# Spacing the side work of a hybrid decoder's first projection, and starting one output norm a product later

## The chip, the cores and the metric

The kernel runs on one core of a Trainium2 chip. The metric is the device time of one execution in microseconds. Three runs of the kernel before gave 2690.6 us as the median (2689.2 to 2692.82).

## What is computed

One inference step of a decoder layer, in fp32, for a prompt of 2048 tokens and 8 samples of 8 tokens each (64 more columns), with model width 1024. Cut to what matters here:

```python
mod = silu(c) @ w_ada + b_ada                      # 6 vectors of shifts, scales, gates
h = rmsnorm(x, norm_mix_w) * (1 + sc1) + sh1
qkv, z, b, a, sq, sk, sv = split(h @ w_in)
qkv = silu(causal_dwconv(qkv, width 4))            # q, k, v of the gated DeltaNet
q, k = l2norm(q) * 128 ** -0.5, l2norm(k)
mix = concat(gated_delta(q, k, v, z, b, a), window_attention(sq, sk, sv))
x = x + g1 * (mix @ w_out)
h = rmsnorm(x, norm_ffn_w) * (1 + sc2) + sh2
gate, up = split(causal_dwconv(h @ w_up, width 3) + conv_b)
x = x + g2 * ((silu(gate) * up) @ w_down)
y = rmsnorm(x, final_norm_w)
```

`l2norm(t)` is `t * rsqrt(sum(t * t) + EPS)`. The outputs are y for both groups, and the new states and caches.

## The kernel before

Channels lie on the 128 partitions and tokens along the free dimension. Every large product is done with each operand split into a high half `hi` (rounded to a shorter fp32 form) and a low half `lo` (the remainder): three matmuls, hi x hi, hi x lo and lo x hi, make one step (`gemm_steps`, L319; the matmul is L324). For a weight tile, ScalarE casts the high half (L315) and another engine subtracts to get the low one (L316). The tokens are treated in two halves, `hf` = 0 and 1, each in three blocks `bi` of up to 384 columns.

**Order of the work.** The program writes generators. `beside(steps, filler, share)` (L334) runs one step of side work, then `share` steps of a filler, which is a projection; `lockstep` (L343) takes one step of each of its chains in a pass. The Tile framework then schedules the instructions by this priority and by its own simulated times, so that an engine's final order can differ from the program's. Each engine runs its queue in order. All loads and stores are issued on SP's queue. `tc.issue_after(loads[-1])` keeps a load behind the last weight load.

**The first input projection** (the end of the main part, up to `first.close()`). Two of its 22 row tiles, m = 0 and 1, are made during the start. Then `inproj(0, h, ic, range(2, 12))` is the filler: 10 tiles x 3 blocks x 8 steps = 240 steps, over five PSUM banks in turn. The first 28 steps run alone; then `beside(tasks, filler, SHARE[3])` with `SHARE[3]` = 8.0 adds two chains in lockstep:

- `ada_cols` (L171), eight groups of four loads `wada` of 512 KB, each with 64 small matmuls (L181), a copy by ScalarE (L184) and transposes (L188), two steps a group; then `weight_sums` of six units (L1577), three steps each: loads of `suv`, four VectorE sums, stores to `ws_d` that the down projection reads much later.
- `bias_tables` (eight steps), `gates` (eleven steps), and three times `x_rstd` (L269): the squares of the second token half are summed in `xacc` (four steps), then `token_rstd` (L205) adds over the partitions with a matmul into `ss_ps` (L214), VectorE and GpSimd make 1/rms (`rsq` L142, `rtok` L143), VectorE makes one diagonal matrix `dg` for each 128 tokens (L218), and after a `yield` a matmul with ones spreads them over the partitions (`rb_ps`, L222), which ScalarE copies (L224).

The evacuation `in_evac` (L571) of a tile m < 12 runs the convolution (`conv_block`, L515; the taps are L531 on VectorE) and `silu2` (L542):

```python
nc.scalar.activation(t, x, AF.Tanh, scale=0.5)                          # L545
nc.vector.scalar_tensor_tensor(x, t, 1.0, x, ALU.add, ALU.mult)         # L546
```

It gives twice the silu. `front` (L622), which normalises q and k for each chunk of 128 tokens, undoes the factor 2: it adds 4 EPS to the sums of squares and halves one of its norms. Tiles 12 to 21 of the first half (z, and the attention's q, k, v) are a later filler, beside the first chunks. For odd m, GpSimd makes the low half of an input weight, for even m VectorE.

**Down** (`down_phase`, L1604). A Strassen-like scheme of seven products (`DOWN`: A11 B11, S2 T2, S3 T3, S1 T1, S4 B22, A22 T4, A12 B21), done for the first and the second part (`ip` = 0 and 1) of both token halves, which are the groups 2 and 1. A product takes eleven steps i of four accumulators; four or eight of the eight PSUM banks, in the rotating list `free`, hold them. T2 and T4 are made on the fly from two loads each (`tr`, `tx`, L1668); the others are loaded as they are. `norm` (L1693) is the final RMSNorm of one group of columns: `token_rstd`, then the products with 1/rms by VectorE (L1717) and GpSimd (L1714), and the stores of y. One step of it is taken after each step i from 1 to 7 of the product that it lies beside. For `ip` = 0, group 2's norm is made after product j = 4 and runs beside j = 5 (A22 T4), in the banks `free[4:6]`; for `ip` = 1 its arguments are kept in `late` and it runs one product later, in `free[-2:]`. Group 1's norms are late already.

Of the kernel before, what the change touches and what calls it, by code (L numbers as in the profile page):

```python
# [17 lines left out]
AF = mybir.ActivationFunctionType  # L18
# [11 lines left out]
NCH = L // P  # L30
# [4 lines left out]
EPS = 1e-6  # L35
# [6 lines left out]
PW, SW = L // 4, L // 8  # L42
# [52 lines left out]
def kernel(  # L95
# [5 lines left out]
    nc = tc.nc  # L101
# [103 lines left out]
    def token_rstd(accs, n, dst, pool, bank):  # L205


        ps = bank("ss_ps")
        r = pool.tile([P, 4], F32, tag="rtok", name="rtok")

        cuts = [min(t, n - P) for t in range(0, n, P)]
        for j, t in enumerate(cuts):
            for i, a in enumerate(accs):
                nc.tensor.matmul(ps[:, j:j + 1], a[:, t:t + P], ones[:, 0:1], start=i == 0, stop=i == len(accs) - 1)  # L214
        rsqrt(pool, r[:, :len(cuts)], ps[:, :len(cuts)], 1.0 / D, len(cuts))
        dg = pool.tile([P, len(cuts), P], F32, tag="sq", name="dg", bufs=2)
        for j, t in enumerate(cuts):
            nc.vector.tensor_scalar_mul(dg[:, j], ident, r[:, j:j + 1])  # L218
        yield True
        bp = bank("rb_ps")  # L220
        for j, t in enumerate(cuts):
            nc.tensor.matmul(bp[:, t:t + P], ones, dg[:, j], start=True, stop=True)  # L222
        if dst is not None:
            nc.scalar.copy(dst[:, :n], bp[:, :n])  # L224
        yield True
# [43 lines left out]
    def x_rstd(hf, bi, rB, pool, bank):  # L269

        c0, n = HALVES[hf][bi]
        acc = pool.tile([P, HB[0]], F32, tag="xacc", name="xacc", bufs=2)[:, :n]
        for k in range(KT):
            x = pool.tile([P, HB[0]], F32, tag="xst", name="xst", bufs=5)[:, :n]
            with tc.issue_after(loads[-1]):
                nc.sync.dma_start(x, I["xT"][k, :, c0:c0 + n])
            nc.scalar.activation(x if k else acc, x, AF.Square)
            if k:
                nc.gpsimd.tensor_tensor(acc, acc, x, ALU.add)
            if k % 2:  # L280
                yield True
        yield from token_rstd([acc], n, rB, pool, bank)

    def first_rstd(bi, xs, rB, pool, bank, eng):

# [24 lines left out]
    def load_split(src, eng=None, out=None):  # L310
        return split(load_raw(src), eng, out)
# [37 lines left out]
    def chain(*gens):  # L349
        for g in gens:  # L350
            yield from g
# [5 lines left out]
    def project(ms, src, load, hb, hf, evac, after=None, freed=None, tags=("acc",), turn=(2, 2), third=None, w0=None):  # L357


        order = list(pairs(ms, turn))  # L360
        new = [m for i, (m, _) in enumerate(order) if m not in [x for x, _ in order[:i]]]
        first = max(2, turn[0])
        w = {m: w0 if w0 and not i else (load, third)[i == 2](m) for i, m in enumerate(new[:first])}
        new = new[first:]
        last = {bi: i for i, (_, bi) in enumerate(order)}
        for i, (m, bi) in enumerate(order):
            ps = bank(src, tags[i % len(tags)])
            yield from gemm_steps(ps, w[m], hb[bi], HALVES[hf][bi][1])
            if bi == 2 and new:
                w[new[0]] = load(new[0])  # L370
                new.pop(0)
            evac(m, bi, ps)
            if bi == 2 and after:
                after(m)
            if freed and last[bi] == i:
                freed(bi)
# [138 lines left out]
    def conv_block(ps, n, np_, hist, state, w, bias, dst):  # L515
# [23 lines left out]
            nc.gpsimd.tensor_copy(state, sb[:, :, NT_S:])  # L539
        return rb  # L540

    def silu2(x, rb):  # L542

        t = rb[:, :x.shape[1]]
        nc.scalar.activation(t, x, AF.Tanh, scale=0.5)  # L545
        nc.vector.scalar_tensor_tensor(x, t, 1.0, x, ALU.add, ALU.mult)  # L546
# [24 lines left out]
    def in_evac(hf, bi, m, ps, ic):  # L571
        c0, n = HALVES[hf][bi]
        np_ = n - LS if c0 + n == LT else n
        ev = evp[0].tile([P, 512], F32, tag="cv", name="ev", bufs=evp[2])[:, :n]
        if m < 12:
            o = ic["out"]
            rb = conv_block(ps, n, np_, o[:, m, 0:3], b8(o[:, m, 3:27]), ic["cw"][:, m], None, ev)
            silu2(ev, rb)
        elif m < 16:
            nc.scalar.activation(ev, ps[:, :n], AF.Tanh, scale=0.5)  # L580
            nc.vector.scalar_tensor_tensor(ev, ev, 1.0, ps[:, :n], ALU.add, ALU.mult)
            nc.gpsimd.tensor_scalar(ev, ev, ic["dnw"], 1.0, ALU.mult, ALU.mult)
        elif m < 20:
            nc.scalar.mul(ev, ps[:, :n], -0.125)
        else:
            nc.scalar.copy(ev, ps[:, :n])
        nc.sync.dma_start(proj[m, :, c0:c0 + n], ev)
        if m == 20 and c0 + n == LT:
            nc.sync.dma_start(O["p_swa_k"], ev[:, np_ - P:np_])
            nc.sync.dma_start(O["s_swa_k_new"], ev[:, np_:])  # L590

    def inproj(hf, h, ic, ms, **kw):
        return project(ms, "in_ps", lambda m: load_split(I["w_inT"][m], nc.gpsimd if m % 2 else nc.vector), h, hf,
                       lambda m, bi, ps: in_evac(hf, bi, m, ps, ic), **kw)


# [25 lines left out]
    def front(c, d, pool, rows=P):  # L622
# [15 lines left out]
        ss = pool.tile([P, H, 2], F32, tag="ss", name="ss")  # L638
        kq_ps = []
        for i in range(2):  # L640
            ps = heads(bank(f"kq_ps{i}", "fr"))
            kq_ps.append(ps)
            for h in range(H):
                nc.tensor.transpose(ps[:rows, h, :], kq[:, h, i, :], ident)
            for h in range(H):
                jk = pool.tile([P, P], BF16, tag="junk", name="junk", bufs=1)
                nc.scalar.activation(jk[:rows], ps[:rows, h, :], AF.Square, accum_out=ss[:rows, h, i:i + 1])
            yield True

        nc.vector.tensor_scalar_add(ss[:rows], ss[:rows], 4 * EPS)  # L650
        nr = pool.tile([P, H, 2], F32, tag="nr", name="nr", bufs=1 if smp else 3)
        nc.gpsimd.tensor_tensor(nr[:rows], ss[:rows], halves[:rows], ALU.pow)
        bn = pool.tile([P, 2, H], F32, tag="bn", name="bn")
# [10 lines left out]
        Dc = pool.tile([P, H, rows], F32, tag="gm", name="Dc", bufs=2)  # L664
        nc.scalar.activation(Dc[:rows], d_ps[:rows, :H * rows].rearrange("p (h i) -> p h i", h=H), AF.Exp)
        nc.gpsimd.tensor_tensor(Dc[:rows], Dc[:rows], over_h(tle, rows), ALU.mult)
        nc.vector.tensor_scalar_mul(nr[:rows, :, 0], nr[:rows, :, 0], 0.5)
        nc.vector.tensor_scalar_mul(nr[:rows, :, 1], nr[:rows, :, 1], float(128.0 ** -0.5))
        yield True
        v_ps = bank("v_ps", "fr")  # L670
# [906 lines left out]
    def weight_sums(units, pool):  # L1577

        tt = nc.vector.tensor_tensor
        cut = lambda t: (t[:, :D // 2], t[:, D // 2:])  # L1580
        for i in units:
            uv = pool.tile([P, 2, D], F32, tag="suv", name="suv", bufs=1)
            for x, k in enumerate((K1[i], K2[i])):
                with tc.issue_after(loads[-1]):
                    nc.sync.dma_start(uv[:, x], I["w_downT"][k])
            (a11, a21), (a12, a22) = cut(uv[:, 0]), cut(uv[:, 1])
            yield True
            tt(a22, a21, a22, ALU.add)
            tt(a21, a11, a21, ALU.subtract)
            tt(a11, a22, a11, ALU.subtract)  # L1590
            tt(a12, a12, a11, ALU.subtract)
            yield True
            for x in range(2):
                nc.sync.dma_start(ws_d[KH * x + i], uv[:, x])
            yield True
# [8 lines left out]
    def down_phase(ds, dr, pd):  # L1604
# [4 lines left out]
        free = [pd.tile([P, 512], F32, tag=f"d{i}", name="dn_ps", bufs=1) for i in range(8)]  # L1609
        free = [free[i] for i in (3, 4, 2, 1, 0, 5, 6, 7)]  # L1610
# [116 lines left out]
        finish = None  # L1727
        for q in range(Q):
            ip, j = divmod(q, ND)
            wn, tn, g, new, outs = DOWN[j]  # L1730
            last = q == Q - 1
            if j == 0:
                x, sums = {}, {}
            cols = {1: slice(LH + PW * ip, LH + PW * ip + wide(q, 1)), 2: slice(PW * ip, PW * ip + PW)}
# [4 lines left out]
            if new:  # L1739

                acc = dict(zip(order, free))
# [67 lines left out]
                    r = subs[s]  # L1809
                    finish = norm(1, r.start, r.stop - r.start, x, sums[1], cols[1], [acc[0, 1], acc[1, 1]], True)  # L1810

            if j == 4 and not ip:
                finish = norm(2, 0, PW, x, sums[2], cols[2], free[4:6], wait=2)
            elif j == 4:
                late = (2, 0, PW, x, sums[2], cols[2])
            elif j == 5 and ip:
                finish = norm(*late, free[-2:])
            elif j == 6:
                late = (1, 0, PW, x, sums[1], cols[1])
            elif j == 2 and ip:  # L1820
                finish = norm(*late, free[-2:], wait=2)
# [6 lines left out]
    XST = 9  # L1828
    PLAN = [(3, 1), (3, 1), (3, 1, 2), (3, 4, 4, 2), (3, 4, 4, 2), (3, 4, 5, 5), (3, 4, 5, 5), (3, 4, 5)]
    HB = (384, 384, 320)  # L1830
    SHARE = (8.0, 2.0, 6.0, 8.0, 2.0, 5.0, 2.0, 8.0)
    PLAIN = 3

    gate = cp.tile([P, NCH + 1, H], F32, tag="gate", name="gate")
# [9 lines left out]
    with ExitStack() as main:  # L1844
# [10 lines left out]
        with ExitStack() as es:  # L1855
# [79 lines left out]
            for bi in range(3):  # L1935
                for m in range(2):
# [2 lines left out]
        rBs = [rB_tile(bi) for bi in range(3)]  # L1939
        at_bank = lambda name: bank(name, "at")  # L1940
        tasks = lockstep(
            chain(*[ada_cols([(c, k + q) for q in range(4)], ac, st, at_bank) for c in range(2, 6) for k in (0, 4)],
                  weight_sums(range(6), sa)),
            chain(bias_tables(sa), gates(0, h, ic["wb"], ip), *[x_rstd(1, bi, rBs[bi], sa, st_bank) for bi in range(3)]))
        zero_images(sa)
        filler = inproj(0, h, ic, range(2, 12), tags=("acc", "acc", "fr", "fr", "at"), turn=(0, 0), w0=w2)
# [188 lines left out]
```

## Time and profile before

| | |
|---|---|
| median of three runs | 2690.6 us |
| the profiled execution | 2689.79 us |
| its span, first to last instruction | 2688.0 us |
| TensorE (PE) busy | 2606.4 us, 97% |
| VectorE (DVE) busy | 1899.5 us, 71% |
| ScalarE (ACT) busy | 1305.9 us, 49% |
| GpSimd (POOL) busy | 788.2 us, 29% |
| mean granted TensorE clock | 0.990 |
| mean HBM traffic | 162 GB/s |

How to read it: an engine is busy while an instruction of it is in flight, and for TensorE, whose matmuls overlap, that is not the same as running at its peak. Times in the views count from the span's start. In a row of instructions, the part behind the bar or in brackets is the idle time of the engine just before, and the instruction that ended it. A wait for several semaphores is put down to the last. "PEclk" is the share of full clock that TensorE was granted in the stretch.

### The profile page before, as it was taken

What the parts mean: (1) busy time and instruction counts of PE and PEld (TensorE: products, weight loads), DVE (VectorE), ACT (ScalarE), POOL (GpSimd) and SP (SyncE); (2) the same over time, 40 slices, a digit from 0 to 9 for tenths busy, and PEclk for the clock granted to TensorE, in tenths of its full rate; (3) what the DMA queues carried; (4) which work ended last, traced back from release to release, by engine and by line L of the source; (5) the groups of instructions that cost most, each with busy time, mean ns of one, the idle gap of its engine ahead of it and who ended that gap; (6) DMA issues with size and microseconds to landing.
All of it is one profiled execution on the core that took longest, in us unless ns stands there. A gap on an engine that the chain in (4) does not pass through costs nothing.

```text
span 2688.0 us, 50078 instructions
## 1 busy us (share of the span) xinstructions
PE 2606.4 (97%) x18344; PEld 2403.3 (89%) x18344; DVE 1899.5 (71%) x3933; ACT 1305.9 (49%) x3404; POOL 788.2 (29%) x682
## 2 busy tenths in 40 slices
PE   7998999999999999999999999999999999999998
PEld 5898988788999998888898899999999997879988
DVE  7667579888523778898868565786776666676676
ACT  6444255555233555455553454555555554444343
POOL 2024243343222412222211113345555520020022
PEclk9999989999999999999999999999999999999999
DMA  7677444232256542333245337324555458677673
GB/s 281 229 266 247 123 144 117 78 96 83 92 146 202 178 141 78 96 99 88 74 155 186 117 111 253 130 82 156 171 168 174 172 181 297 213 248 246 224 244 131
DMA packets 318660, 438.07 MB, mean 163 GB/s; under 512 B 83107, under 2 KB 221572, under 8 KB 318148
## 3 DMA queue, kind: packets, MB, share of 16 engines
q1 hardware_dynamic: 318412, 434.85, 49.6%
q8 instruction: 144, 2.36, 0.4%
q14 instruction: 104, 0.85, 0.1%
HBM read 320.44 MB, written 115.33 MB: 162 GB/s over the span
## 4 chain that ended last, share of the span: by engine, by line
PE 57%; DMA 5%; DVE 4%; issue 2%; POOL 2%; ACT 1%; SPq 0%; POOLq 0%; DVEq 0%; ACTq 0%
PE up_ps L324 20%; PE dn_ps L1751 13%; PE op_ps L324 5%; PE uq_b L1541 4%; PE uq_c L1541 2%; PE in_ps L324 2%; PE uq_g L1541 2%; PE uq_u L1541 2%; DMA tr<-T_d 1%; DMA rawu<-in_w_upT_dram 1%; PE uq_a L1541 1%; PE pv_ps L971 1%; DMA rawg<-in_w_upT_dram 1%; PE as_ps L934 1%; DVE w_lo L316 1%
## 5 line engine op out<-in xcount | busy, mean ns | idle before, releaser
L324 PE MATMUL up_ps<-hi,w_hi 128*128 128x384 f32 (+2 forms) x1152 | 377.0, 327 | 0.0
L324 PE MATMUL up_ps<-hi,w_lo 128*128 128x384 f32 (+2 forms) x1152 | 370.4, 322 | 0.6 <-DVE w_lo L316 0.6
L324 PE MATMUL up_ps<-lo,w_hi 128*128 128x384 f32 (+2 forms) x1152 | 370.7, 322 | 0.0
L324 PE MATMUL in_ps<-hi,w_hi 128*128 128x384 f32 (+2 forms) x1056 | 346.7, 333 | 3.8 <-ACT hi L265 1.1
L324 PE MATMUL in_ps<-lo,w_hi 128*128 128x384 f32 (+2 forms) x1056 | 347.6, 330 | 2.2 <-DVE lo L266 1.3
L324 PE MATMUL in_ps<-hi,w_lo 128*128 128x384 f32 (+2 forms) x1056 | 346.8, 329 | 1.3 <-POOL w_lo L316 1.3
L1751 PE MATMUL dn_ps<-th,wh 128*128 128x512 f32 (+2 forms) x796 | 273.1, 344 | 4.9 <-DVE x L1219 4.0
L1751 PE MATMUL dn_ps<-tl,wh 128*128 128x512 f32 (+2 forms) x796 | 273.2, 343 | 3.6 <-DVE tl L1643 3.6
L1751 PE MATMUL dn_ps<-th,wl 128*128 128x512 f32 (+2 forms) x796 | 272.3, 344 | 0.0
L324 PEld LDWEIGHTS up_ps<-hi,w_hi 128*128 128x128 f32 x1152 | 217.4, 189 | 15.9 <-issue 10.2
L324 PEld LDWEIGHTS up_ps<-lo,w_hi 128*128 128x128 f32 x1152 | 217.5, 189 | 8.6 <-issue 7.3
L324 PEld LDWEIGHTS up_ps<-hi,w_lo 128*128 128x128 f32 x1152 | 217.3, 189 | 8.7 <-issue 6.4
L324 PEld LDWEIGHTS in_ps<-hi,w_hi 128*128 128x128 f32 x1056 | 199.7, 190 | 18.2 <-issue 10.2
L324 PEld LDWEIGHTS in_ps<-lo,w_hi 128*128 128x128 f32 x1056 | 201.0, 190 | 11.0 <-issue 4.5
L324 PEld LDWEIGHTS in_ps<-hi,w_lo 128*128 128x128 f32 x1056 | 201.0, 190 | 8.3 <-issue 4.9
L316 DVE TENSOR_TENSOR w_lo<-w_raw,w_hi 128x1024 fp32r<-128x1024 f32 x111 | 140.7, 1268 | 83.2 <-ACT w_hi L315 82.2
L315 ACT CAST w_hi<-w_raw 128x1024 fp32r<-128x1024 f32 x132 | 138.0, 1046 | 119.6 <-PE in_ps L324 39.2
L531 DVE SCALAR_TENSOR_TENSOR ev<-rb,cw,ev 128x384 f32<-128x384 f32 (+1 forms) x216 | 147.3, 688 | 34.0 <-ACT ev L524 31.4
L1751 PEld LDWEIGHTS dn_ps<-th,wh 128*128 128x128 f32 x796 | 151.7, 191 | 21.9 <-ACT wh L1642 2.5
L1751 PEld LDWEIGHTS dn_ps<-tl,wh 128*128 128x128 f32 x796 | 151.6, 190 | 19.7 <-DVE tl L1643 3.9
L1751 PEld LDWEIGHTS dn_ps<-th,wl 128*128 128x128 f32 x796 | 151.4, 190 | 15.7
L1642 ACT CAST wh<-wr 128x512 fp32r<-128x512 f32 x149 | 92.1, 618 | 149.4 <-PE dn_ps L1751 119.6
(545 smaller groups left out, 6728.2 us busy)
## 6 DMA issues: line engine op xcount, KB each, us to landing
w_raw<-in_w_upT_dram SPq DMA_DIRECT2D x50, 512.0 KB
wada<-in_w_ada_dram SPq DMA_DIRECT2D x44, 512.0 KB
w_raw<-in_w_inT_dram SPq DMA_DIRECT2D x44, 512.0 KB
wr<-ws_d SPq DMA_DIRECT2D x88, 256.0 KB
w_raw<-in_w_outT_dram SPq DMA_DIRECT2D x40, 512.0 KB
proj<-ev SPq DMA_DIRECT2D x88, 192.0 KB
d<-act_d SPq DMA_DIRECT2D x33, 512.0 KB
wr<-in_w_downT_dram SPq DMA_DIRECT2D x66, 256.0 KB
```

Of the source, the lines that this page charges most:

```text
L315: nc.scalar.copy(hi, raw)
L316: (eng or nc.vector).tensor_tensor(lo, raw, hi.bitcast(F32), ALU.subtract)
L324: nc.tensor.matmul(ps[:, :n], a[:, k, :], b[:, k, :n], start=first is not False and k == ks[0] and i == 0, stop=last is not False and k == ...
L531: nc.vector.scalar_tensor_tensor(out, src(j), w[:, j:j + 1], out, ALU.mult, ALU.add)
L934: nc.tensor.matmul(banks[v][:, 256 * g + P * k0:256 * g + 256], a[r, g0 + g], b[r, keys], start=i == 0, stop=i == 2, tile_position=(64 * v ...
L971: nc.tensor.matmul(pv_ps[64 * v:64 * v + 64, :], (vprev[0], vt)[half][:, 64 * v:64 * v + 64], PT[v, half], start=half == k0, stop=half == 1)
L1541: nc.tensor.matmul(bk[t][:, :nb], u[:, k], v[:, k], start=new and k == 0 and y == 0, stop=k == KG - 1 and y == 2, skip_group_check=True)
L1642: nc.scalar.copy(h, raw)
L1751: nc.tensor.matmul(acc[m, s][:, :n], w[q, i][a][:, c], th[b][:, v], start=new and i == 0 and y == 0, stop=i == KH - 1 and y == 2, skip_gro ...
```

## The change

- The steps of the ada groups and of the weight sums in the first projection are spread over two passes each, the two steps of each `token_rstd` there over four; the filler's share falls from 8.0 to 3.1 steps a pass.
- For the first half of the tokens, `in_evac` uses Silu itself on ScalarE in place of Tanh and the VectorE step. The factor is then 1 and not 2, and `front` takes it from `TWICE` by chunk: EPS in place of 4 EPS, and no halving.
- In the first half, VectorE makes the low halves of all input weights; in the second half it stays as it was.
- In down, group 2's norm of `ip` = 0 is made after j = 5 and not j = 4, as for `ip` = 1, with two yields for each pair of rows as before. It uses `free[-2:]`.

```diff
@@ x_rstd
-        yield from token_rstd([acc], n, rB, pool, bank)
+        yield from spaced(token_rstd([acc], n, rB, pool, bank))
+
+    def spaced(steps, n=4):
+
+        for _ in steps:
+            for _ in range(n):
+                yield True
@@
+    TWICE = (1, 2)
+
     def silu2(x, rb):
@@ in_evac
-            silu2(ev, rb)
+            if TWICE[hf] == 2:
+                silu2(ev, rb)
+            else:
+                nc.scalar.activation(ev, ev, AF.Silu)
@@ inproj
-        return project(ms, "in_ps", lambda m: load_split(I["w_inT"][m], nc.gpsimd if m % 2 else nc.vector), h, hf,
+        return project(ms, "in_ps", lambda m: load_split(I["w_inT"][m], nc.gpsimd if hf and m % 2 else nc.vector), h, hf,
@@ front
-        nc.vector.tensor_scalar_add(ss[:rows], ss[:rows], 4 * EPS)
+        f = TWICE[c >= NCH // 2]
+
+        nc.vector.tensor_scalar_add(ss[:rows], ss[:rows], f * f * EPS)
@@ front
-        nc.vector.tensor_scalar_mul(nr[:rows, :, 0], nr[:rows, :, 0], 0.5)
+        if f != 1:
+            nc.vector.tensor_scalar_mul(nr[:rows, :, 0], nr[:rows, :, 0], 1.0 / f)
@@ down_phase
-            if j == 4 and not ip:
-                finish = norm(2, 0, PW, x, sums[2], cols[2], free[4:6], wait=2)
-            elif j == 4:
+
+            if j == 4:
                 late = (2, 0, PW, x, sums[2], cols[2])
-            elif j == 5 and ip:
-                finish = norm(*late, free[-2:])
+            elif j == 5:
+                finish = norm(*late, free[-2:], wait=2 - ip)
@@
-    SHARE = (8.0, 2.0, 6.0, 8.0, 2.0, 5.0, 2.0, 8.0)
+    SHARE = (8.0, 2.0, 6.0, 3.1, 2.0, 5.0, 2.0, 8.0)
@@
-            chain(*[ada_cols([(c, k + q) for q in range(4)], ac, st, at_bank) for c in range(2, 6) for k in (0, 4)],
-                  weight_sums(range(6), sa)),
+            chain(*[spaced(ada_cols([(c, k + q) for q in range(4)], ac, st, at_bank), 2) for c in range(2, 6) for k in (0, 4)],
+                  spaced(weight_sums(range(6), sa), 2)),
```

## Prediction

> **What bounds the kernel now.** I read the page first, then the stretches of the span (busy time of each engine, granted clock, DMA), then the waits of TensorE in the two places that the change touches, and the order of time around them.
>
> ```profile
> span 2688.0 us, 50078 instructions
> PE 2606.4 (97%) x18344; PEld 2403.3 (89%) x18344; DVE 1899.5 (71%) x3933; ACT 1305.9 (49%) x3404; POOL 788.2 (29%) x682
> ```
>
> TensorE has a matmul in flight for 2606.4 of 2688.0 us. The change removes no matmul. Time can come only from the 82 us in which TensorE is idle, and from stretches in which its clock is granted at half. The profiled run took 2689.79 us, 1.8 more than its span and 0.8 below the median of 2690.6; I sum against 2689.79 and add the 0.8 at the end. The rows below give, for a stretch: its length, busy time of PE, its weight loads, DVE, ACT and POOL, then granted clock, DMA share and GB/s.
>
> ```profile
> 82.00:173.00 91.00, 88.22 (x882) 75.51 (x878) 47.23 (x96) 37.72 (x103) 4.74 (x2) 1.00 0.78 274
> 82.00:247.00 165.00, 153.42 (x1333) 138.79 (x1329) 112.36 (x197) 78.85 (x213) 40.70 (x29) 0.97 0.74 259
> 209.00:247.00 38.00, 29.20 (x172) 27.90 (x172) 35.28 (x52) 19.26 (x55) 19.55 (x15) 0.87 0.71 250
> 221.00:231.20 10.20, 6.17 (x20) 5.80 (x21) 9.91 (x14) 4.90 (x13) 7.90 (x7) 0.50 0.93 333
> 2370.00:2400.00 30.00, 25.59 (x113) 20.76 (x112) 26.16 (x35) 13.31 (x24) 11.79 (x8) 0.94 0.70 229
> 2388.40:2391.80 3.40, 3.40 (x11) 2.77 (x10) 3.40 (x5) 1.72 (x3) 2.04 (x2) 0.50 0.57 188
> ```
>
> The first projection with its side work fills 82 to 247 us. In its last 38 us TensorE is idle 38.00 - 29.20 = 8.80 us while VectorE is busy 35.28 of 38; in its first 91 us VectorE is busy only 47.23. The side work is lopsided. From 221.0 to 231.2 the clock is granted at 0.50: the 6.17 us of matmuls there would take half at full clock, so 3.09 us more are lost. In down's place TensorE is idle 30.00 - 25.59 = 4.41 us, and 3.40 us of matmuls run at half clock, 1.70 us lost.
>
> ```profile
> PE rb_ps L222 <- DVE dg L218: 7.5, 3, 6.7
> PE in_ps L324 <- POOL w_lo L316: 1.3, 1, 1.3
> PE dn_ps L222 <- DVE dg L218: 3.6, 1, 3.6
> ```
>
> These waits (the first two from 200 to 260 us, the last from 2360 to 2410; total, times, longest) name the same culprit twice: the matmul that spreads 1/rms over the partitions waits for the diagonals `dg` that VectorE makes from `ss_ps`.
>
> **Part 1, the spacing in the first projection.**
>
> ```profile
> 210.43 0.39 PE L214 MATMUL ss_ps<-ones,xacc 128*128 128x1 f32 x3
> 224.50 0.77 PE L222 MATMUL rb_ps<-dg,ones 128*128 128x128 f32 x2 [6.73 <-DVE dg L218]
> 221.97 0.15 DVE L142 TENSOR_SCALAR rsq<-ss_ps 128x3 f32<-128x3 f32 x1
> 223.47 1.07 DVE L218 TENSOR_SCALAR dg<-cst,rtok 128x128 f32<-128x128 f32 x2 [0.22 <-POOL rtok L143]
> 82.00:173.00 91.00, 56.23 (x335) 52.49 (x336) 0.00 (x0) 13.95 (x33) 1.00 0.78 274
> ```
>
> The sums leave TensorE at about 211, but VectorE comes to them at 221.97, behind conv taps and weight sums. The work proper is short: 221.97 to the start of the first `dg` is 1.5 us. Between sums and spread the program puts one step of side work, with 8 of the filler's steps. A filler step is three matmuls, and 335 matmuls took 56.23 us (last row, `in_ps` alone), so a step is 0.50 us: 4 us of cover for a queue of 11. After the change there are 4 passes at 3.1, so 12.4 steps, 6.2 us, and other side work besides.
>
> More decides than that cover. Before, the two chains are 34 and 37 passes long, and at 8 steps each the 212 filler steps left after the first 28 are gone after 26.5 passes: one norm and two and a half weight sums pile up at the end. After, the ada and weight-sum chain has 2 x 34 = 68 passes, the other 8 + 11 + 3 x 12 = 55, and 68 x 3.1 = 211 steps: the filler lasts to the end, and the last norm is done 13 passes before it. The first norm's sums move from the 23rd of 26.5 passes to about the 23rd of 68, into the stretch where VectorE is half idle. I take the 8.80 + 3.09 = 11.89 us as won but for 0.9 us, about the second and third waits left over from 7.5 - 6.7 above: **-11.0 us**, bounds -11.9 (no wait left) and 0 (the wait stays).
>
> What it brings forward: eight groups of four ada loads. In program order the eight groups took 16 passes with 128 filler steps; now 32 passes with 99. That is 29 x 0.50 = 14 us less between first and last.
>
> ```profile
> PE ada_ps L181 <- DMA wada<-in_w_ada_dram: 1.1, 2, 0.9
> DMA packets 1360, 3.40 MB, mean 340 GB/s; under 512 B 154, under 2 KB 759, under 8 KB 1359
> 160.40:173.20 12.80, 12.80 (x133) 11.60 (x132) 5.13 (x15) 3.72 (x10) 0.00 (x0) 1.00 0.93 348
> ```
>
> Now they wait 1.1 us in all. From 82 to 173 us 274 GB/s flowed, 24.9 MB; in some 78 us the same bytes need 320 GB/s, just under the 340 that ran at 96 to 106 us with the engines nearly full and the 348 of the last row, at share 0.93. So the last three groups, which no longer have the bias tables and gates beside them, will sometimes arrive late. The four buffers of `wada` refill only as the previous group's matmuls end. Bounds: 0, and all 14 us. I take **+2.5 us**, near the 0-end because the measured rate covers the need. Behind a waiting ada matmul stand the projection's matmuls on TensorE; everyone waits. The weight sums' loads and stores and the x loads, all on SP's queue, move later, out of the way of ada; the last weight sums still have no reader before down.
>
> **Part 2, Silu, and the low halves of the weights.**
>
> ```profile
> L546 DVE SCALAR_TENSOR_TENSOR ev<-rb,ev 128x384 f32<-128x384 f32 (+1 forms) x30 | 17.6, 588 | 9.4 <-ACT rb L545 9.2
> L316 DVE TENSOR_TENSOR w_lo<-w_raw,w_hi 128x1024 fp32r<-128x1024 f32 x4 | 4.9, 1220 | 2.1 <-ACT w_hi L315 2.1
> L545 ACT ACTIVATE rb<-ev 128x384 f32<-128x384 f32 (+1 forms) x30 | 14.6, 488 | 44.9 <-DVE ev L531 44.8
> L1260 ACT ACTIVATE rB<-rB x9: 463/525/527, 1720.9 to 1784.8; 128x384 f32<-128x384 f32 x6, 128x320 f32<-128x320 f32 x3
> ```
>
> VectorE loses 30 second halves of silu, 17.6 us, and gains five low halves (m = 3 to 11) at 1220 ns, 6.1 us: 11.5 us lighter, out of 112.36. The other five (m = 13 to 21) fall into 250 to 350 us. GpSimd no longer makes any here, so the 1.3 us wait for `w_lo` (already inside the 8.80) has no cause left. Silu itself costs ScalarE what Tanh cost (525 ns at L1260; 488 is the mean over 384 and 256 columns). What is dearer is its table:
>
> ```profile
> 179.27 0.22 ACT L446 ACTIVATE t<-t 128x32 f32<-128x32 f32 x1
> 179.59 1.28 ACT L447 ACT_TABLE_LOAD   x1
> 180.88 0.23 ACT L447 ACTIVATE t<-t 128x32 f32<-128x32 f32 x1
> 1719.44 1.28 ACT L1260 ACT_TABLE_LOAD   x1
> ```
>
> Exp and Tanh share a table here (no load between them at 179), Silu needs its own (load before L1260). The gates' Exp come in four clusters amid the evacuations, each now with a load in and one out, one more for Ln, one at each end of the stage: 11 loads for today's 2, 9 x 1.28 = 11.5 us on ScalarE, which is idle 165.00 - 78.85 = 86 us in the stage. Five PSUM banks take the filler in turn, 8 steps or 4 us each, so one load is covered. I take **+0.5 us** on the path; bounds 0 and 11.5. The rule against this edit is in the Trainium skill, "ScalarE: Activation LUTs", section "Table sets: the hidden batching unit": batch calls by set; its cost section states a drain of about 1380 ns beside each load. By that, an estimate of 9 x 2.66 = 24 us on ScalarE, still under its idle time. The trace disagrees on the drain: Ln starts 0.01 us after its load ends. The key norm of the first eight chunks loses one small multiply each: nothing.
>
> **Part 3, down's first norm one product later.**
>
> ```profile
> 2384.21 0.69 DVE L1668 TENSOR_TENSOR tr<-tr,tx 128x512 f32<-128x512 f32 x1 [2.32 <-issue]
> 2386.03 0.15 DVE L142 TENSOR_SCALAR rsq<-dn_ps 128x4 f32<-128x4 f32 x1
> 2387.31 0.88 DVE L218 TENSOR_SCALAR dg<-cst,rtok 128x128 f32<-128x128 f32 x4 [1.13 <-POOL rtok L143]
> 2542.25 0.95 PE L214 MATMUL dn_ps<-ones,dsum 128*128 128x1 f32 x8
> 2549.99 1.05 PE L222 MATMUL dn_ps<-dg,ones 128*128 128x128 f32 x8
> 2639.64 0.95 PE L214 MATMUL dn_ps<-ones,dsum 128*128 128x1 f32 x8
> 2645.52 1.05 PE L222 MATMUL dn_ps<-dg,ones 128*128 128x128 f32 x8
> ```
>
> The norm now runs beside A22 T4, whose right side is a sum of two loads; VectorE idles 2.32 us there and takes `rsq` behind that. One product later, beside A12 B21, there is no such sum, and the squares are summed a whole product earlier. The last two pairs are the two norms that already run a product late: neither spread waits. So 4.41 + 1.70 = **-6.1 us**, bounds -6.1 and 0. What moves along: four SP stores of y, four GpSimd products, four VectorE products. With two yields each they reach three steps into the next product:
>
> ```profile
> L1714 POOL TENSOR_TENSOR x<-x,drB 128x512 f32<-128x512 f32 x4 | 7.1, 1797 | 2.5 <-ACT drB L224 2.5
> L1717 DVE SCALAR_TENSOR_TENSOR x<-x,nw,drB 128x512 f32<-128x512 f32 x4 | 6.9, 1778 | 0.0
> 2404.00:2432.00 28.00, 28.00 (x126) 23.18 (x125) 17.80 (x25) 15.81 (x29) 5.15 (x4) 1.00 0.83 280
> ```
>
> In that product (last row) VectorE has 10 us and GpSimd 23 us free for 7 each. The banks (now the last two of the product just ended, not the first two) are evacuated before the next product's second step. Free.
>
> **Sum.** -11.0 + 2.5 + 0.5 - 6.1 = -14.1. Profiled 2689.8 - 14.1 = 2675.7; with the 0.8, **2676.5 us**.
>
> ```profile
> 350.00:400.00 50.00, 45.23 (x357) 40.34 (x357) 43.38 (x90) 32.32 (x96) 22.54 (x17) 0.86 0.48 149
> PE pt_ps L961 <- DVE nl L954: 1.5, 1, 1.5
> ```
>
> An unknown of about 3 us either way: at 350 to 400 us no wait exceeds 1.5 us, yet the clock averages 0.86, so 7 us of matmul time ran at half grant. That stage starts earlier and may meet the gate better or worse. The Trainium skill, "TensorE: Matmul & The Clock Gate", section "HAM oscillation", puts the danger at idle gaps above about 3.4 us; by that the new ada waits cost only their length. This stretch shows that short waits close together halve the clock too.
>
> **Rivals.** *The spread still waits.* `al`'s Exp ran at 31.88 us, far ahead of its place in the program:
>
> ```profile
> 31.88 0.20 ACT L438 ACTIVATE al<-al 128x4 f32<-128x4 f32 x1
> ```
>
> So each engine's order is not the program's, and spacing may not reach it; then only down's 6.1 and about 1 us from `w_lo` remain, and with +2.5 the time is 2686. Against it: the sums now do stand where 8 steps a pass put them. 0.14. *Down's wait only moves*: 2682.6. 0.07; the two late norms speak against. *ScalarE's table loads reach TensorE* in full: 2676.5 + 11.0 = 2687.5. 0.06; against it, the five banks. *Slower: ada starves.* If compressed loads cannot beat today's pace, TensorE loses the 14 us in seven waits of 2 us; if each also brings 3.4 us of half clock (as at 2388), 7 x 1.7 = 12 us more: 2676.5 - 2.5 + 26 = 2700. It decides from the point where the stage's rate stays under 274 GB/s. 0.07; the 348 speaks against.
>
> **How the numbers follow.** Forecast 0.66, its own range 2668 (all 18.0 won, nothing paid, the later gate 3 us better, half of the early idle 91.00 - 88.22 gone) to 2682. About 5.4 us, 0.2%, is what a measurement can tell from no change. Faster by more (below 2685.2): 0.66 + 0.07 + a third of the first rival 0.05 = 0.78. Within: the rest of it and the table rival 0.15. Slower: 0.07. The range 2668 to 2687 leaves out the starved case, most of the table rival and a tail of the forecast.
>
> **What would show it.** Right: no wait of `rb_ps` for `dg` over 1 us before 250 us, full clock from 205 to 235, VectorE's busy share level over the stage; no wait at down's first spread, clock 1.00 there; some `wada` waits of a microsecond. Wrong: the 6 us wait standing elsewhere, `wada` waits over 8 us in sum, or waits of `in_ps` for `w_hi` behind table loads.

## The result, and the profile after

The changed kernel took 2672.55 us (median of four runs, 2670.2 to 2675.07) against 2691.71 for the kernel before beside it (2689.2 to 2699.4): ratio 0.9924, 95% interval 0.9902 to 0.9947. The forecast was 2676.5. Between the medians the step is 19.2 us (14 to 26 by the interval), where the sum had 14.1. Between the two profiled runs it is 2689.79 - 2675.07 = 14.7 us; the profiled run of the changed kernel is the slowest of its four, so the nearness of 14.7 to 14.1 is in part chance. The shares of the sum did not come out, as the sections below show.

The page of the changed kernel begins:

```profile
span 2673.3 us, 50044 instructions
PE 2602.2 (97%) x18344; PEld 2400.5 (90%) x18344; DVE 1870.6 (70%) x3899; ACT 1311.3 (49%) x3411; POOL 764.2 (29%) x672
```

TensorE's instructions are the same number; 34 fewer on VectorE. The first projection (from the first ada matmul beside the filler to the first `kq_ps`), whole in the kernel before and then in stretches of the changed kernel (length, busy PE, PEld, DVE, ACT, POOL, clock, DMA share, GB/s):

```profile
81.90:259.70 177.80, 166.22 (x1419) 151.59 (x1419) 118.90 (x213) 81.86 (x218) 46.51 (x38) 0.97 0.74 259
```

```profile
82.90:251.50 168.60, 163.06 (x1392) 146.50 (x1392) 96.84 (x184) 84.30 (x217) 30.70 (x32) 0.98 0.77 269
205.00:235.00 30.00, 30.00 (x194) 30.00 (x193) 18.88 (x32) 13.31 (x36) 0.00 (x0) 1.00 0.60 204
236.00:242.00 6.00, 1.07 (x7) 0.75 (x6) 3.46 (x8) 0.80 (x2) 0.00 (x0) 0.88 0.57 221
240.50:247.30 6.80, 5.34 (x25) 5.34 (x26) 3.85 (x8) 0.82 (x3) 4.73 (x7) 0.50 0.75 258
2360.00:2390.00 30.00, 30.00 (x134) 24.85 (x133) 23.21 (x33) 17.08 (x30) 5.14 (x4) 1.00 0.74 236
```

Where TensorE stood before, at 205 to 235 us, it is now busy throughout, at full clock. But a new hole stands at 236 to 242, with 6.8 us of half clock behind it. In the stretch of down that the change touches (last row) no idle time is left and the clock is full. TensorE's waits of the changed kernel from 82 to 252 us:

```profile
PE in_ps L330 <- DVE ev L593: 4.9, 1, 4.9
PE ada_ps L181 <- DMA wada<-in_w_ada_dram: 0.6, 1, 0.6
```

The wait for `dg` is gone, the ada loads cost 0.6 us, and one wait that the prediction did not have costs 4.9. The order of time on TensorE for sums and spread (the first norm of the first projection, then down's):

```profile
165.94 0.72 PE L214 MATMUL ss_ps<-ones,xacc 128*128 128x1 f32 x6
170.59 0.83 PE L222 MATMUL rb_ps<-dg,ones 128*128 128x128 f32 x6
2393.66 0.95 PE L214 MATMUL dn_ps<-ones,dsum 128*128 128x1 f32 x8
2400.91 1.05 PE L222 MATMUL dn_ps<-dg,ones 128*128 128x128 f32 x8
```

None has a bracket: nothing was waited for. The new hole, in VectorE's and SP's order of time in the changed kernel:

```profile
233.34 0.81 SPq L1599 DMA_DIRECT2D suv<-in_w_downT_dram  x2
...
235.74 0.48 DVE L537 SCALAR_TENSOR_TENSOR ev<-rb,cw,ev 128x256 f32<-128x256 f32 x1
238.76 0.69 DVE L1602 TENSOR_TENSOR suv<-suv 128x512 f32<-128x512 f32 x1 [2.54 <-DMA proj<-ev]
239.37 0.48 DVE L537 SCALAR_TENSOR_TENSOR ev<-rb,cw,ev 128x256 f32<-128x256 f32 x1
239.76 0.68 DVE L1603 TENSOR_TENSOR suv<-suv 128x512 f32<-128x512 f32 x1
240.36 0.47 DVE L537 SCALAR_TENSOR_TENSOR ev<-rb,cw,ev 128x256 f32<-128x256 f32 x1
240.76 0.68 DVE L1604 TENSOR_TENSOR suv<-suv 128x512 f32<-128x512 f32 x1
241.36 0.54 DVE L593 SCALAR_TENSOR_TENSOR ev<-ev,in_ps 128x384 f32<-128x384 f32 x1
```

VectorE stops at 236.2 in front of the last weight sum (L1602), whose load SP issued at 233.34. The releaser is named as another DMA that ended then; where the same stop shows in `spacing_only` and `pool_low`, it is the sum's own load. Behind the sum in VectorE's queue stand the taps of tile 11, two more sums and the evacuation of the first z tile (L593), which reads its PSUM bank; TensorE waits for that bank. TensorE stops at 237.0, so of its 4.9 us the stop at the load takes 1.7 and the queue behind it the rest.

**Lost time.** From here on, "lost" in a stretch is TensorE's idle time there plus half of the matmul time that ran at half clock. The clock part can be checked against (1 - clock) x length, coarsely, since the clock has two digits and that product counts idle time too. In the first projection: before, 11.6 + 3.1 = 14.7 us; after, 5.5 + 2.7 = 8.2. In down: 28.8 before, 20.7 after. Over the whole span 101.1 and 87.5: 13.6 of the 14.7 us are accounted for. The mixers of the first half (its DeltaNet and attention, from the first `as_ps` to the first `op_ps`) lost 21.4 before and 20.8 after.

### The profile page after: what moved, and what is told of

Its sections match the earlier page's. It is cut to its first block, busy times and chain, and to the rows that moved or that the text cites. A ratio compares the mean times of both kernels' runs of the same rounds, so it can differ in the third digit from the quotient of the medians.

```text
span 2673.3 us, 50044 instructions
## 1 busy us (share of the span) xinstructions
PE 2602.2 (97%) x18344; PEld 2400.5 (90%) x18344; DVE 1870.6 (70%) x3899; ACT 1311.3 (49%) x3411; POOL 764.2 (29%) x672
## 5 line engine op out<-in xcount | busy, mean ns | idle before, releaser
L322 DVE TENSOR_TENSOR w_lo<-w_raw,w_hi 128x1024 fp32r<-128x1024 f32 x121 | 152.5, 1261 | 93.1 <-ACT w_hi L321 92.8
L537 DVE SCALAR_TENSOR_TENSOR ev<-rb,cw,ev 128x384 f32<-128x384 f32 (+1 forms) x216 | 136.9, 643 | 30.3 <-ACT ev L530 28.2
```

The costliest lines, as they stand in the source:

```text
L322: (eng or nc.vector).tensor_tensor(lo, raw, hi.bitcast(F32), ALU.subtract)
L537: nc.vector.scalar_tensor_tensor(out, src(j), w[:, j:j + 1], out, ALU.mult, ALU.add)
```

## The experiments

Each ratio is to the kernel before on the same chip. The table collects them; "order" is VectorE's instruction order in the mixers as the framework scheduled it, with the same letter where 99.9% or more agrees. In the traces TensorE, ScalarE and GpSimd too keep their order in the mixers where the letter is the same (over 99%), and most change it where the letter differs, so a letter stands for a whole schedule.

| kernel | lost in first projection | lost in mixers | order | median us | ratio (95%) |
|---|---|---|---|---|---|
| before | 14.7 | 21.4 | A | | 1 |
| after | 8.2 | 20.8 | B | 2672.55 | 0.9924 (0.9902 to 0.9947) |
| down_only | 15.4 | 16.8 | A | 2686.94 | 0.9979 (0.9969 to 0.9988) |
| first_only | 4.8 | 17.9 | B | 2676.71 | 0.9939 (0.9925 to 0.9953) |
| no_spacing | 6.9 | 37.6 | C | 2694.28 | 1.0008 (0.9998 to 1.0019) |
| spacing_only | 17.8 | 21.0 | A | 2692.74 | 1.0007 (0.9996 to 1.0018) |
| tanh_back | 11.3 | 20.4 | D | 2679.37 | 0.9955 (0.994 to 0.997) |
| pool_low | 7.2 | 23.7 | E | 2677.19 | 0.9952 (0.9935 to 0.9968) |
| no_norm_spacing | 6.9 | 22.7 | B | 2672.57 | 0.9933 (0.9916 to 0.9951) |
| five_sums | 0.2 | 30.8 | F | 2676.68 | 0.995 (0.9933 to 0.9966) |
| norm_spaced_55 | 12.8 | 19.9 | B | 2677.08 | 0.9948 (0.9934 to 0.9961) |
| norm_spaced_60 | 9.4 | 36.1 | C | 2697.13 | 1.0014 (1.0003 to 1.0025) |
| five_sums_4 | 6.3 | 20.5 | B | 2672.23 | 0.9933 (0.992 to 0.9946) |
| silu_low_pool | 9.9 | 23.7 | E | 2679.44 | 0.9959 (0.9945 to 0.9973) |

The lost times are of one profiled run each. Kernels with the same code in a stretch differ by 3 to 5 us there (after and first_only in the first projection, before and down_only in the mixers), so only larger steps are read.

**Down alone**, `down_only`: the kernel before with the new `j == 5` branch.

> The kernel before with only down's norm one product later. Theory: the 3.6 us wait of the spread for dg and the 0.8 us wait for dsum at 2376 to 2388 us vanish with the 3.4 us of half clock behind them: 6.1 us off, ratio 0.9977 to before; no wait at that norm's spread. Rival (the wait only moves into the next product): ratio 0.9995 to 1.0005 and a wait of 2 to 4 us at the spread, 25 to 30 us later.

Measured 0.9979, as the theory had it. The norm's sums and spread in its trace, and the 60 us around:

```profile
2405.41 0.95 PE L214 MATMUL dn_ps<-ones,dsum 128*128 128x1 f32 x8
2412.66 1.05 PE L222 MATMUL dn_ps<-dg,ones 128*128 128x128 f32 x8
```

```profile
2360.00:2420.00 60.00, 60.00 (x275) 49.96 (x274) 46.82 (x66) 31.57 (x56) 16.69 (x12) 1.00 0.72 236
```

No wait, no idle time, full clock. The wait did not move.

**The first projection alone**, `first_only`: the changed kernel with the old branch back.

```diff
-            if j == 4:
+            if j == 4 and not ip:
+                finish = norm(2, 0, PW, x, sums[2], cols[2], free[4:6], wait=2)
+            elif j == 4:
                 late = (2, 0, PW, x, sums[2], cols[2])
-            elif j == 5:
-                finish = norm(*late, free[-2:], wait=2 - ip)
+            elif j == 5 and ip:
+                finish = norm(*late, free[-2:])
```

> The changed kernel with down's norm put back beside A22 T4, so the first projection's edits alone. Theory: the two places are independent and add up: 6 us slower than the changed kernel, 12 to 13 us faster than before (ratio about 0.9953), the wait at down's spread back at about 3.6 us. Rival: what down gained comes from arriving earlier, not from the later norm: no wait there and the changed kernel's time.

Measured 0.9939, a little better than the 0.9953 expected; the waits in down are back, shared out differently:

```profile
PE dn_ps L214 <- POOL dsum L1245: 2.0, 1, 2.0
PE dn_ps L222 <- DVE dg L218: 1.9, 1, 1.9
```

0.9939 x 0.9979 = 0.9918 against 0.9924 for both: the two places add up.

**Without the spacing**, `no_spacing`: the changed kernel with the three `spaced(...)` taken off and `SHARE[3]` = 8.0.

> The changed kernel without the spacing and with 8.0 filler steps a pass again; Silu, the low halves on VectorE and down's later norm stay. Theory (the level side work brings the first stage's gain): the side work piles up at the end again, rb_ps waits 3 us or more for dg between 205 and 225 us; 6 to 9 us slower than the changed kernel, ratio about 0.995 to before. Rival (VectorE's 11.5 us lighter load is enough): no wait over 1 us and a time within 2 us of the changed kernel.

Measured 1.0008: slower than either side had it, although down's gain is still in it. Its first projection's waits:

```profile
PE rb_ps L222 <- DVE dg L218: 4.2, 1, 4.2
PE ada_ps L181 <- DMA wada<-in_w_ada_dram: 0.4, 1, 0.4
```

The wait for `dg` is back, as the theory said, but it is nearly all that the stage loses: 6.9 us, no more than with spacing. The time went elsewhere. The mixers of this kernel, then of the changed one:

```profile
354.60:826.70 472.10, 448.64 (x3481) 393.32 (x3481) 333.91 (x920) 216.27 (x708) 157.07 (x133) 0.97 0.35 101
```

```profile
356.80:810.80 454.00, 439.08 (x3482) 386.10 (x3482) 327.24 (x920) 213.85 (x710) 157.03 (x133) 0.98 0.36 105
```

Same work, 18 us longer, and not one line of the change is in it, save a small multiply that both leave out. It is not a matter of when the mixers start: here at 354.6 us, and in `first_only`, which lost 17.9 us there, at 353.5.

**The spacing alone**, `spacing_only`: the changed kernel with these edits and the old branch in down.

```diff
-    TWICE = (1, 2)
+    TWICE = (2, 2)
-        ... load_split(I["w_inT"][m], nc.gpsimd if hf and m % 2 else nc.vector)
+        ... load_split(I["w_inT"][m], nc.gpsimd if m % 2 else nc.vector)
```

> The kernel before with only the spacing and the 3.1 share; Tanh with its VectorE step, low halves of odd tiles on GpSimd and the early norm in down stay. Theory (spacing is the cause): the 6.7 us wait of rb_ps for dg is gone, 7 to 10 us off, ratio about 0.9968. Rival (VectorE is too full without Silu): waits of 3 us or more for dg or for ev stay somewhere in the stage, ratio 0.999 to 1.001.

Measured 1.0007, the rival's number. The waits from 82 to 260 us:

```profile
PE in_ps L330 <- DVE ev L593: 5.8, 1, 5.8
PE adat_ps L188 <- ACT ms L184: 2.5, 1, 2.5
PE rb_ps L222 <- DVE dg L218: 2.4, 2, 2.2
```

Spacing shortens the wait for `dg` by 5.1 us and makes one of 5.8 us for `ev`, behind the last weight sums. By itself it wins nothing. The theory that spacing brings the first stage's gain fell with this and the run before. The next theory: VectorE's load in the stage counts, spacing moves the wait, and the mixers' loss depends on the order that the scheduler happens to give them.

**Silu undone**, `tanh_back`: `TWICE = (2, 2)` alone.

> The changed kernel with Tanh and its VectorE step put back in the first half of the tokens; spacing, low halves on VectorE and down's later norm stay. Theory (VectorE's load in the first projection is what counts, and spacing only moves the wait): TensorE's idle time and half clock from the first ada matmul to the first kq_ps, 8.2 us in the changed kernel, come back to 15 to 20 us, mostly as a wait of in_ps for ev at the stage's end; ratio about 0.997 to before. Rival (spacing carries the gain): 8 to 10 us there, ratio 0.993.

Measured 0.9955; the stage lost 11.3 us, between the two. The waits in its first projection:

```profile
PE in_ps L330 <- DVE ev L593: 5.2, 1, 5.2
PE rb_ps L222 <- DVE dg L218: 1.8, 2, 1.6
PE adat_ps L188 <- ACT ms L184: 1.5, 1, 1.5
```

The wait for `ev` is the changed kernel's (4.9), the wait for `dg` and one for ScalarE's copy are back in part. Taking Silu away costs the stage 3.1 us here, not 7 to 12, and that is no more than the scatter.

**Low halves on GpSimd again**, `pool_low`: the one line of `inproj` undone.

> The changed kernel with the low halves of odd input weights on GpSimd again in the first half. Theory (VectorE's load counts, and GpSimd was not late): VectorE is 6 us lighter in the stage, 5 to 9 us of TensorE's time lost there, within 3 us of the changed kernel, ratio 0.992 to 0.994. Rival (GpSimd's 2.5 us for a low half was a cause of its own, through waits for w_lo and slower VectorE beside it): waits for w_lo of a microsecond or more, 4 us slower or worse.

The stage lost 7.2 us with no wait for `w_lo`: the first is as the theory said. The total, 4.6 us above the changed kernel's by the medians, is over the 3 us expected, though the intervals of the two ratios overlap; the mixers have another order here and lost 23.7. What the low halves do to VectorE shows in the groups of its taps and low halves, changed kernel first, then `pool_low`:

```profile
L537 DVE SCALAR_TENSOR_TENSOR ev<-rb,cw,ev 128x384 f32<-128x384 f32 (+1 forms) x87 | 56.1, 654 | 25.5 <-ACT ev L530 24.2
L322 DVE TENSOR_TENSOR w_lo<-w_raw,w_hi 128x1024 fp32r<-128x1024 f32 x10 | 12.7, 1273 | 5.8 <-ACT w_hi L321 5.8
```

```profile
L537 DVE SCALAR_TENSOR_TENSOR ev<-rb,cw,ev 128x384 f32<-128x384 f32 (+1 forms) x88 | 65.9, 758 | 31.3 <-ACT ev L530 20.3 <-DMA w_raw<-in_w_inT_dram 9.0 <-DMA wada<-in_w_ada_dram 0.6
L322 DVE TENSOR_TENSOR w_lo<-w_raw,w_hi 128x1024 fp32r<-128x1024 f32 x5 | 6.0, 1206 | 1.4 <-ACT w_hi L321 1.4
```

Five low halves more cost VectorE 6.7 us, and its taps, one fewer, cost it 9.8 us less. The trace of `pool_low` shows where: a low half on GpSimd, the tap beside it, and a later tap of the same size.

```profile
208.24 2.50 POOL L322 TENSOR_TENSOR w_lo<-w_raw,w_hi 128x1024 fp32r<-128x1024 f32 x1 [3.71 <-ACT w_hi L321]
208.41 2.76 DVE L537 SCALAR_TENSOR_TENSOR ev<-rb,cw,ev 128x384 f32<-128x384 f32 x1
211.69 0.60 DVE L537 SCALAR_TENSOR_TENSOR ev<-rb,cw,ev 128x384 f32<-128x384 f32 x1
```

The tap that meets the low half lasts until just after it ends. So it is with all five low halves there: one tap each of 2.05 to 2.81 us, where taps with nothing on GpSimd beside them take 0.62 us (384 columns) or 0.48 (256).

**The norm's two steps not spaced**, `no_norm_spacing`: `yield from token_rstd(...)` without `spaced`.

> The changed kernel without the spacing of token_rstd: sums and spread of 1/rms are one pass of 3.1 filler steps apart, 1.6 us; all else stays. Theory (a level VectorE answers in 2 to 4 us, so the cover between the two is the smaller part): three waits of rb_ps for dg of 0 to 2 us, 1 to 4 us slower than the changed kernel. Rival (the cover is the point): waits of 4 us or more with half clock behind them, 10 us slower or more.

Measured 2672.57, the changed kernel's time, at the low end of the theory: the waits for `dg` come to 0.5 us. With VectorE level, the four passes between sums and spread are not needed.

**Five weight sums in place of six**, `five_sums`:

```diff
-                  spaced(weight_sums(range(6), sa), 2)),
+                  spaced(weight_sums(range(5), sa), 2)),
-            beside(lockstep(sample_delta(sp), sample_attend(sp), weight_sums(range(6, KH), sp)), filler, SHARE[2])
+            beside(lockstep(sample_delta(sp), sample_attend(sp), weight_sums(range(5, KH), sp)), filler, SHARE[2])
```

> The changed kernel with five units of weight sums in the first projection and the sixth moved to the sample stage. Theory (the 4.9 us wait of in_ps for ev at 242 us is VectorE standing at the last unit's sums until its load lands, with the evacuation of z queued behind): that wait falls under 1 us and the half clock at 240 to 247 goes: 5 to 7 us faster than the changed kernel, ratio about 0.990. Rival (the wait only moves to the fifth unit, or to the sample stage): within 2 us of the changed kernel.

The first half of the theory held to the letter, the second did not: 0.995. First projection, mixers, and a stretch in the mixers:

```profile
83.90:239.70 155.80, 155.56 (x1362) 139.33 (x1361) 92.14 (x178) 83.00 (x215) 27.34 (x28) 1.00 0.77 269
352.50:813.60 461.10, 448.56 (x3475) 392.43 (x3475) 329.29 (x914) 215.73 (x702) 154.35 (x132) 0.96 0.35 103
593.10:599.90 6.80, 6.77 (x24) 5.71 (x24) 5.70 (x21) 4.85 (x26) 3.75 (x4) 0.50 0.72 220
```

The first projection loses 0.24 us in all: without the last weight sum the new wait is gone. VectorE still stands at the load of the fifth:

```profile
221.87 0.69 DVE L1602 TENSOR_TENSOR suv<-suv 128x512 f32<-128x512 f32 x1 [3.63 <-DMA suv<-in_w_downT_dram]
```

TensorE does not wait for that. The side work now has 62 passes, so 62 x 3.1 = 192 of the 212 filler steps go beside it and some 20 are left behind it. A sum that stands at its load costs TensorE time where the filler ends with it; the run does not separate the two. Then the mixers, with a sixth order, lose 12.5 idle and 18.3 to the clock.

**The order as the only difference in the mixers**, `norm_spaced_55` and `norm_spaced_60`: ada groups and weight sums not spaced, norms spaced, `SHARE[3]` = 5.5 and 6.0. The two shares were chosen because the scheduled order of the mixers is B with the one and C with the other.

> The changed kernel with the ada groups and the weight sums not spaced, the norms' two steps still spaced over four passes, and 5.5 filler steps a pass. VectorE's order in the mixers of the first half (from the first as_ps to the first op_ps) is the changed kernel's. Theory (that order decides, and it follows from the scheduler, not from where side work waits): 17 to 23 us of TensorE's time lost in the mixers, as in the changed kernel, and a total within 4 us of it, ratio 0.992 to 0.994. Rival (the spacing of the ada groups and weight sums is what saves the mixers): 30 us or more lost there and a ratio of 0.998 to 1.001, as without any spacing.

> The same kernel with 6.0 filler steps a pass. VectorE's order in the mixers is now the one without any spacing (a third of it in common with the changed kernel's). Theory: 30 us or more of TensorE's time lost in the mixers, ratio 0.997 to 1.001, 12 to 20 us slower than with 5.5. Rival (the order is not what costs): within 4 us of 5.5.

Measured 0.9948 and 1.0014, both just over what was expected, and 20 us apart. The mixers with 5.5, then with 6.0:

```profile
359.70:812.30 452.60, 440.57 (x3482) 387.42 (x3482) 326.40 (x919) 213.43 (x709) 156.22 (x133) 0.98 0.36 105
```

```profile
356.80:828.10 471.30, 445.94 (x3481) 390.43 (x3481) 332.60 (x919) 217.15 (x710) 157.38 (x133) 0.97 0.35 101
```

18.7 of the 25.1 us between these two profiled runs are there. With 6.0 the longest waits in the mixers are the same as in `no_spacing`:

```profile
PE z_ps L769 <- DVE T L809: 4.4, 2, 2.6
PE d_ps L675 <- ACT junk L659: 4.2, 1, 4.2
PE u_ps L769 <- DVE Y L817: 3.9, 3, 2.5
```

None of these was over 0.7 us in total with 5.5. So the 20 us of `no_spacing` are the price of order C, and a kernel without spaced ada groups and weight sums escapes it when the scheduler gives it order B. That the spacing of those protects the mixers is refuted. And the norms' spacing alone does not keep the spread from waiting: with 6.0, `rb_ps` waited 4.8 us for `dg` in the first projection.

**Five sums with order B**, `five_sums_4`: `five_sums` with `SHARE[3]` = 4.0.

> The kernel with five units of weight sums in the first projection, with 4.0 filler steps a pass in place of 3.1. VectorE's order in the mixers is the changed kernel's again. Theory: the first projection still loses under 2 us, the mixers lose 17 to 23 us and not 31, and the total is 5 to 9 us below the changed kernel: 2664 to 2668 us, ratio 0.989 to 0.991. Rival (the time saved in the first projection is lost in the mixers whatever the order): ratio 0.9935 to 0.996.

The mixers are back at 20.5, as the theory said. The first projection is not: 6.3 us lost.

```profile
PE adat_ps L188 <- ACT ms L184: 2.7, 1, 2.7
PE in_ps L330 <- DVE ev L593: 1.5, 1, 1.5
```

At 4.0 the filler runs out before the side work does, and other waits take the place (the two longest are shown). Median 2672.23, ratio 0.9933 (0.992 to 0.9946): the changed kernel's time. No kernel here is clearly better than the changed one.

**Silu without spacing and low halves**, `silu_low_pool`: the kernel before with `TWICE = (1, 2)` and down's new branch.

> The kernel before with Silu in the first half of the tokens and down's later norm alone: no spacing, low halves of odd tiles on GpSimd. Theory (Silu's 17.6 us off VectorE carry the first projection's gain): idle time and half clock in the first projection 6 to 9 us, against 14.7 before. Rival (the low halves carry it): 13 us or more, with waits for w_lo. The total says little, since the mixers get a fourth order.

The stage lost 9.9 us, just over the 6 to 9 expected and under the rival's 13. Most of it is the old wait:

```profile
PE rb_ps L222 <- DVE dg L218: 6.5, 2, 6.2
PE ada_ps L181 <- DMA wada<-in_w_ada_dram: 0.9, 1, 0.9
```

Silu does not remove the wait for `dg`. What the stage loses besides fell from 14.7 - 7.5 = 7.2 us to 9.9 - 6.5 = 3.4, a step of the size of the scatter.

## Why the prediction was right, and where it was not

The direction was right and the measured time is inside the range: 14.1 us worked out, 19.2 between the medians, 14.7 between the profiles. Step by step:

- **Part 3, down: right.** -6.1 forecast; `down_only` gives (1 - 0.9979) x 2690 = 5.6 us (3.2 to 8.3 by its interval), and no wait in the next product. Reading the two late norms of the kernel before as the model was enough.
- **Part 1, spacing, -11.0: the wait went, another came, and the gain was put down to the wrong edit.** The stage lost 6.5 us less, not 11. What was to go went: 7.5 us for `dg`, 1.3 for `w_lo` and the 3.1 of half clock, and 2.1 us of smaller waits, for the ada loads and for ScalarE's copy, besides. In their place came one wait of 4.9 us with 2.7 of half clock behind it. The step that failed is the sentence that the weight sums move "later, out of the way", costed at nothing because nobody reads them soon. They have no reader, but VectorE executes them in order and stands at their loads. That this is where the 7.6 us arose is read from the trace, and `five_sums` bears it out. And spacing alone won nothing (`spacing_only`).
- **The ada loads, +2.5: too high.** 0.6 us of waits, against 1.1 before; the loads kept up with the shorter pace. The starved case did not come near.
- **Part 2, Silu and low halves, +0.5: the sign was wrong.** Nothing in TensorE's waits of the first projection names a table load. The prediction counted VectorE's 11.5 us of relief and gave it no term. The relief was in fact some 22 us over the stage (118.90 to 96.84), since the taps became faster too, and the gain goes with it: with the spacing in place, Silu and the low halves together take the kernel from 1.0007 (`spacing_only`) to 0.9939 (`first_only`). Between runs that differ in one of the edits, Silu cut the stage's loss in three of three pairs (14.7 to 9.9, 17.8 to 7.2, 11.3 to 8.2), the low halves in two of three (9.9 to 6.9, 17.8 to 11.3, but 7.2 to 8.2), the spacing in one of three (9.9 to 7.2, but 14.7 to 17.8 and 6.9 to 8.2). Most of these steps are no larger than the scatter of 3 to 5 us, so how the gain divides stays open; the low halves alone were not run.
- **The unknown of 3 us at 350 to 400 us: right that the later stage could move, wrong in cause and in how far.** It was named as luck with the clock gate. In this result the mixers moved by 0.6 us. But they hang on their scheduled order: A and B lose 17 to 23 us, C 36 to 38, F 31. The change landed on B, and that was luck: the prediction had no term for it, and with order C much the same gains in the first projection and in down end at 1.0008 (`no_spacing`). The first rival's premise, that engines do not follow the program's order, was right; it bit in the mixers and not at the spread.

So the sum was right partly because an over-sized gain (11.0 for 6.5) stood beside over-sized costs (3.0 for next to none), and because the mixers did not move. What in order C makes the mixers slower was read only as far as the three waits above; which engine's or instruction's place begins it stays open.

## What to carry to other kernels

Work without a reader is not free to move: ask what its engine stands at before it, and what is queued behind. When a framework schedules each engine's order, an edit can be paid or charged in a stage that it does not touch; so compare the stages' idle time and clock, and the scheduled orders, before a total is put down to an edit. Two kernels with the same work in a stage and a different order of it, here by one number, tell the two apart.

## What was not expected of the hardware

- A VectorE tap that meets a low half on GpSimd lasts until the low half ends (2.05 to 2.81 us in `pool_low`, in place of 0.48 or 0.62). With the low halves on GpSimd the taps took 713 to 758 ns in the mean (`spacing_only` 713, before 732, `silu_low_pool` 731, `pool_low` 758); with them on VectorE 634 to 664 (`tanh_back` 634, after 654, `no_spacing` 664). In `pool_low` against the changed kernel the taps win back 9.8 us, more than the 6.7 that the moved work costs.
- The clock can go to half without a long idle gap. TensorE's only wait from 586 to 600 us in `five_sums`, and a row of its order of time:

```profile
PE kq_ps L656 <- DVE AM L697: 0.5, 1, 0.5
```

```profile
592.18 0.43 PE L769 MATMUL z_ps<-T,AM 32*32 32x16 f32 x28
```

  It waited 0.5 us, and yet the clock stood at 0.50 from 593.1 to 599.9 (the row above); just before ran matmuls of small tiles, and whether they are the cause was not tested. The Trainium skill, "TensorE: Matmul & The Clock Gate", section "HAM oscillation", warns of idle gaps over 3.4 us; here the clock halved without such a gap.
- A switch of ScalarE's function table takes 1.28 us. The changed kernel has nine of them from 69 to 258 us, where the kernel before had two, and none shows as a wait of TensorE from 82 to 252 us.
